# Loading the moved copies of the value rows two weight tiles later, with their tap products two splits further on, in a trunk kernel

## The chip, the cores and the metric

The kernel runs on one core of a Trainium2 chip, in one launch. The metric is the device time of that launch in microseconds; lower is better. A core has a matrix engine (TensorE, PE in the profile), a vector engine (VectorE, DVE), a scalar engine (ScalarE, ACT), GpSimd (POOL), and SyncE (SP), which here only issues transfers. Each engine works off its own instruction stream in order; where two engines depend on each other, a semaphore makes one wait. Transfers between the chip's main memory and the on-chip memory are issued by an engine into a queue and moved by 16 DMA engines.

## What is computed

One layer of a hybrid trunk for 256 tokens of width 2048. The parts that matter:

```python
proj = jnp.einsum('bsd,de->bse', rmsnorm(x, norm_mix_w[l]), w_in[l])
q, k, v, z, b_raw, a_raw, p_in, g_a, g_b = jnp.split(proj, splits, axis=-1)
qkv = jax.nn.silu(causal_dwconv(jnp.concatenate([q, k, v], axis=-1), conv_qkv_w[l]))
...
o = gated_delta_rule(q, k, v, g_log, beta)
o = rmsnorm(o, gdn_norm_w[l]) * jax.nn.silu(z.reshape(bsz, seq, N_HEADS, HEAD_DIM))
...
pooled = causal_multiscale_pool(p_in.reshape(bsz, seq, N_POOL_GROUPS, POOL_GROUP_DIM))
y_b = jnp.einsum('bsgc,gcd->bsgd', pooled, pool_w[l]).reshape(bsz, seq, D_POOL) * pool_scale[l]
mixed = jax.nn.sigmoid(g_a) * y_a + jax.nn.sigmoid(g_b) * y_b
x = x + jnp.einsum('bsd,de->bse', mixed, w_out[l])
```

After that comes a gated MLP (width 5632) with its own norms. The change touches the causal convolution of v: `causal_dwconv` over 4 taps is a sum of the rows of v, moved down by 0, 1, 2 and 3 tokens, each times its tap.

```python
def causal_dwconv(x, w):
    width = w.shape[0]
    seq = x.shape[1]
    xp = jnp.pad(x, ((0, 0), (width - 1, 0), (0, 0)))
    y = xp[:, 0:seq] * w[0]
    for j in range(1, width):
        y = y + xp[:, j:j + seq] * w[j]
    return y
```

## The kernel before

**Weights.** All large products read their weights in tiles of 256 x 512. A tile is loaded into `raw` (4 buffers, 512 KB each, SP's queue, L179), cast by ScalarE to its high half `whi` (L258), and VectorE subtracts that from the tile to get the low half `wlo` (L266). This subtraction is called the split; `splits` lists them in order, and "split 231" is the 231st. `whi` and `wlo` have 3 buffers each. `weights()` hands out a tile and begins the tile two further on; `last_load` is the most recent weight load.

**Gemms of the mixers.** `gemm_a` takes one tile at a time. For each it issues 12 matmuls on 128x512: high by high (L301), activations' low by weights' high (L302) and activations' high by weights' low (L303). After each half tile it calls `side()`, which takes one step of a generator, the side work. At the second tile of each gemm (`c == 1`) it first runs what stands in the list `later`.

**Order of the work.** The 16 heads are taken in 4 groups `g`. A group runs its gemms in this order: k, q, v, the pooling mixer's input (p), the gate GB, z and the pool product (in group 3 the pool product stands before z), and the gate GA; each is 8 tiles, the pool product 2. After the four groups comes the output projection. A scheduler that simulates the program decides the order of the instructions on each engine. It goes by the order in which the program states them and by readiness, with two exceptions: `tc.issue_after(x)` holds an instruction behind instruction x, and within `tc.manual_schedule` (from group 3's GA gemm to the output projection's first part) TensorE keeps the order in which the program states its work. In that stretch `ending` opens the last steps of group 3's side work.

**The value path.** `evict` (L714) copies a gemm's result from its bank to the tile `ev` (one buffer). The banks of `gemm_a`, `psm`, are two, taken in turn. For v, `ev` is written to memory (`vrow`, L1055). At the second tile of the next gemm, `v_moved` multiplies it by the last tap into `vt` (L735) and loads the three moved copies from `vrow` (L740): two take the buffers with the tag `cy`, which the convolutions of k and q also use, and one a buffer of its own, `mv`. Later `v_conv`, a part of the side work, multiplies each copy by its tap (L749) and adds it to `vt` (L750). Each product is held behind a split: the n-th behind the split with index `splits_of[g] + n`, and 3 later in group 0. `splits_of[g]` is the count of splits begun at the time of `v_moved`.

**The delta chain** (`gdn`, the side work of a group). Its steps, in order: decay differences (`crow`), Gram matrices on TensorE (L834, L836) with their diagonals (L839), the scaled blocks `ga0` and `ga1` (L853 to L858), their diagonal blocks out to memory (`cdd`, L872) and back (`lb`, L875), and a triangular solve in 31 steps on VectorE (L898, L900) with splits between. The result goes to memory (`tbd`, L905) and back (`TT`, L908), VectorE transposes it to `T` (L920), and TensorE reads it (L944). From there on come more products and merges, up to the group's output, which is gated (L1137, L1139), transposed (L346, copied to `mhi` and `mlo`) and kept as the output projection's operand. The steps of `v_conv` are the last of the side work before `T`, and the conv of q runs beside the first steps.

**The pooling mixer.** In group 3 the pooled values are made by 16 band matmuls (`banded`, L1072, L1074) from `ev`; ScalarE copies them to the high half `phi` (L1077) and VectorE makes the low half `plo` (L1078). They are what the pool product multiplies. `gate` (L1110) evicts a gate's gemm through a tanh, and `yb` (L1115) scales it.

Of the kernel before, what the change touches and what calls it, by code (L numbers as in the profile page):

```python
# [14 lines left out]
P = 128  # L15
S = 256
# [19 lines left out]
def kernel(  # L36
# [20 lines left out]
    nc = tc.nc  # L57
# [11 lines left out]
    def nm(s):  # L69
        cnt[0] += 1  # L70
        return f"{s}_{cnt[0]}"
# [90 lines left out]
    last_load = [None]  # L162
    last_split = [None]
    splits = []
    HALVES = 2

    def weights(ahead=AHEAD):

        begin(taken[0] + ahead + 1)
        taken[0] += 1  # L170
        return made[taken[0] - 1]
# [105 lines left out]
    def side():  # L277
        next(side_work[0], None)
# [5 lines left out]
    def pm():  # L284
        return psm.tile([P, 2, 512], F32, tag="m", name=nm("psm"))


    later = []

    def gemm_a(lh, ll, nk, steps=None, ps=None):  # L290

        ps = pm() if ps is None else ps
        for c in range(nk // 2) if steps is None else steps:
            if c == 1:
                while later:
                    later.pop(0)()
            hi, lo = weights()
            for kk in range(2):
                k = 2 * c + kk
                for t in range(2):  # L300
                    mm(ps[:, t, :], lh(k, t), hi[:, kk, :], start=(k == 0), stop=False)  # L301
                    mm(ps[:, t, :], ll(k, t), hi[:, kk, :], start=False, stop=False)  # L302
                    mm(ps[:, t, :], lh(k, t), lo[:, kk, :], start=False, stop=(k == nk - 1))  # L303
                side()
        return ps
# [395 lines left out]
    SH = 3  # L701
    vrow = dpool.tile([4, SH + S, 512], F32, tag="vrow", bufs=1, name="vrow")
# [28 lines left out]
    splits_of = {}  # L731

    def v_moved(e, g, vt):

        nc.vector.tensor_tensor(vt, e, taps_of[g][3], op=ALU.mult)  # L735
        moved_of[g] = []
        splits_of[g] = len(splits)
        for j in (1, 2, 3):
            m = mp.tile([P, 2, 512], F32, name=nm("mv"), **(dict(tag="cy", bufs=2) if j < 3 else dict(tag="mv")))
            nc.sync.dma_start(m, vrow[g, SH - j : SH - j + S, :].rearrange("(t p) d -> p t d", p=P))  # L740
            moved_of[g].append(m)

    def v_conv(g, vt):

        vt = vt.rearrange("p t h d -> p t (h d)")
        for n, (j, m) in enumerate(zip((2, 1, 0), moved_of[g])):

            with tc.issue_after(splits[splits_of[g] + n + (3 if g == 0 else 0)]):
                nc.vector.tensor_tensor(m, m, taps_of[g][j], op=ALU.mult)  # L749
            nc.vector.tensor_tensor(vt, vt, m, op=ALU.add)  # L750
            yield
        th = mp.tile([P, 2, 512], F32, tag="th", name=nm("th"))
        nc.scalar.activation(th, vt, AF.Tanh)
        yield
        nc.vector.scalar_tensor_tensor(vt, th, 1.0, vt, op0=ALU.add, op1=ALU.mult)
        yield
# [271 lines left out]
    for g in range(4):  # L1028
        kq = mp.tile([P, 4, 2, S], F32, tag="kq", bufs=1, name=nm("kq"))
        for kind, dst in ((1, kq[:, :, 0, :]), (0, kq[:, :, 1, :])):  # L1030
            ps = ps_k0 if kind == 1 and g == 0 else gemm_a(xh, xl, KD)
            e = evict(ps)
            convs.append(conv_silu(e, kind, g, dst))
            if g:
                later.append(lambda conv=convs[-1]: sum(1 for _ in conv))
            elif kind:

                later.append(lambda conv=convs[-1]: side_work.__setitem__(0, chain(conv, running_sums())))
            else:
                later.append(drain)  # L1040
# [3 lines left out]
        res = []  # L1044
        later.append(lambda g=g, kq=kq, vt=vt, res=res, conv=convs[-1]: side_work.__setitem__(
            0, along(gdn(g, kq, vt, v_conv(g, vt), res), conv)))
        v_taps(g)
        if g == 0:
# [3 lines left out]

            later.append(after_k)
        e = evict(gemm_a(xh, xl, KD), rsh)
        nc.sync.dma_start(vrow[g, SH : SH + S, :].rearrange("(t p) d -> p t d", p=P), e)  # L1055
        later.append(lambda e=e, g=g, vt2=vt2: v_moved(e, g, vt2))


        win = WINDOWS[g]
        psb = scales(g)  # L1060
        ps = gemm_a(xh, xl, KD)
        e = evict(ps) if g == 3 else evict(ps, rsh)
        phi = mtile(g, [P, 4, S], F32R, nm("phi"))
# [362 lines left out]
    def lh(k, t):  # L1426
        return at(hhi)(k, t)

    def ll(k, t):
        return at(hlo)(k, t)  # L1430
# [25 lines left out]
    for hf in range(2):  # L1456
# [11 lines left out]
        for n, step in enumerate(steps[hf]):  # L1468
# [11 lines left out]
            if step[0] == "plain":  # L1480
                kp, c = step[1], step[2] % 2
# [133 lines left out]
```

## Time and profile before

| | us |
|---|---|
| median of 3 runs | 1556.24 |
| lowest and highest of them | 1553.46, 1556.99 |
| profiled execution | 1555.57 |
| its span | 1553.9 |
| TensorE busy | 1537.2 |
| VectorE busy | 1195.2 |
| ScalarE busy | 828.8 |

The profile is that of one execution. A row of a timeline begins with the start and the duration in microseconds, then comes the engine, the line of the program, the operation, output and inputs, their shapes and how often it stands there in a row. Square brackets give the idle time before it on its engine and what ended it. In a group row, "x864 | 339.7, 393 | 1.4 <-DVE wlo L266 1.4" says that 864 instructions took 339.7 us, 393 ns each, and that the engine was idle for 1.4 us ahead of them, ended by VectorE's `wlo`. Matmuls are pipelined, so a matmul of 393 ns can be followed by the next one 0.23 us later. A row of the waits names the waiting engine and line, what it waited for, the total in microseconds, the times and the longest. A row of the chain of waits gives start, duration and what the end of the program hung on then. A row of the windows gives the stretch, its length, the engine's busy time and count, the granted clock of TensorE (1.00 is full), the DMA share and GB/s.

### The profile page before, as it was taken

The page shows a single profiled execution, that of the slowest core. Times are in us where ns is not written, and L with a number is a line of the kernel's source. Part 1 is how long each engine was busy: PE and PEld are TensorE (multiplying, and loading weights), DVE is VectorE, ACT ScalarE, POOL GpSimd, SP SyncE. Part 2 cuts the span into 40 slices and gives each one's busy share as a digit, 9 for nine tenths or more (in the row PEclk, how much of TensorE's full clock was granted, in tenths as well). Part 3 has the DMA queues.
Part 4 walks back from the last instruction along what each step waited for, and adds up shares of the span by engine and source line. Part 5 has one row for each costly group of instructions (what it writes and reads, how often), then busy time and mean ns, then how long its engine had stood idle before and what let it go on. Part 6 is the DMA issues. An engine that isn't in the chain of part 4 may idle for free.

```text
span 1553.9 us, 20103 instructions
## 1 busy us (share of the span) xinstructions
PE 1537.2 (99%) x7350; PEld 1268.1 (82%) x7350; DVE 1195.2 (77%) x1712; ACT 828.8 (53%) x1038; POOL 53.6 (3%) x66
## 2 busy tenths in 40 slices
PE   9999999999999999999999999999999999999998
PEld 8878888788878888888887888888888888788786
DVE  6789858996689858886665877777777776878775
ACT  6445446454545446454554656656666655555552
POOL 1010002000100000000000000000000000000000
PEclk9999999999999999999999999999999999999999
DMA  8777757776576756675667555556666558556562
GB/s 273 211 222 211 199 157 223 218 205 177 171 235 206 200 167 203 219 205 178 225 212 245 181 187 186 163 192 204 202 203 203 180 173 284 190 176 204 203 210 89
DMA packets 168018, 310.45 MB, mean 200 GB/s; under 512 B 19267, under 2 KB 23139, under 8 KB 167791
## 3 DMA queue, kind: packets, MB, share of 16 engines
q1 hardware_dynamic: 159456, 287.37, 59.9%
q0 software_dynamic: 3264, 12.58, 2.4%
q10 hardware_dynamic: 5198, 9.23, 1.9%
q8 instruction: 57, 0.93, 0.2%
q14 instruction: 43, 0.34, 0.1%
HBM read 301.75 MB, written 7.38 MB: 199 GB/s over the span
## 4 chain that ended last, share of the span: by engine, by line
PE 95%; DMA 2%; DVE 1%; issue 1%; ACT 1%; POOL 0%; POOLq 0%; ACTq 0%; DVEq 0%
PE psg L1324 29%; PE psm L303 14%; PE psm L301 14%; PE psm L302 14%; PE psm L1309 7%; PE psg L1309 6%; PE psm L444 1%; PE psm L1381 1%; PE psg L346 1%; PE psm L1324 1%; DMA vrow<-ev 1%; PE psg L834 1%; DVE wlo L266 1%; DMA mv<-vrow 1%; DMA raw<-in_w_down_dram 0%
## 5 line engine op out<-in xcount | busy, mean ns | idle before, releaser
L258 ACT CAST whi<-raw 128x1024 fp32r<-128x1024 f32 x460 | 483.9, 1053 | 482.0 <-PE psm L302 273.4
L266 DVE TENSOR_TENSOR wlo<-raw,whi 128x1024 fp32r<-128x1024 f32 x458 | 556.5, 1221 | 167.7 <-ACT whi L258 162.3
L303 PE MATMUL psm<-wlo,xhl 128*128 128x512 f32 x864 | 339.7, 393 | 1.4 <-DVE wlo L266 1.4
L301 PE MATMUL psm<-whi,xhl 128*128 128x512 f32 x864 | 338.6, 392 | 0.0
L302 PE MATMUL psm<-whi,xhl 128*128 128x512 f32 x864 | 337.9, 391 | 0.0
L1324 PE MATMUL psg<-whi,fhl 128*128 128x512 f32 x1208 | 302.1, 390 | 0.4 <-ACT whi L258 0.4
L1324 PEld LDWEIGHTS psg<-whi,fhl 128*128 128x128 f32 x1208 | 225.8, 188 | 47.4 <-ACT whi L258 1.2
L266 DVE TENSOR_TENSOR wlo<-quad,whi 128x1024 fp32r<-128x1024 f32 x112 | 137.1, 1224 | 75.4 <-ACT whi L258 72.1
L303 PEld LDWEIGHTS psm<-wlo,xhl 128*128 128x128 f32 x864 | 162.3, 188 | 35.7 <-DVE wlo L266 2.6
L302 PEld LDWEIGHTS psm<-whi,xhl 128*128 128x128 f32 x864 | 162.3, 188 | 33.4
L301 PEld LDWEIGHTS psm<-whi,xhl 128*128 128x128 f32 x864 | 162.3, 188 | 33.3 <-issue 0.2
L258 ACT CAST whi<-quad 128x1024 fp32r<-128x1024 f32 x112 | 118.1, 1055 | 105.0 <-PE psg L1324 55.9
L1324 PE MATMUL psg<-wlo,fhl 128*128 128x512 f32 x604 | 163.9, 389 | 0.0
L1324 PEld LDWEIGHTS psg<-wlo,fhl 128*128 128x128 f32 x604 | 113.4, 188 | 23.5
L1309 PE MATMUL psm<-wlo,hhi 128*128 128x512 f32 (+1 forms) x150 | 58.1, 387 | 1.1 <-DVE wlo L266 1.1
L1309 PE MATMUL psm<-whi,hhi 128*128 128x512 f32 (+1 forms) x150 | 58.1, 387 | 0.0
L1309 PE MATMUL psm<-whi,hlo 128*128 128x512 f32 (+1 forms) x150 | 57.9, 386 | 0.0
L198 DVE TENSOR_TENSOR quad<-quad 128x1024 f32<-128x1024 f32 x40 | 49.0, 1225 | 9.1 <-DMA quad<-in_w_up_dram 8.0
L1309 PE MATMUL psg<-whi,hhi 128*128 128x512 f32 (+1 forms) x130 | 50.4, 388 | 2.3 <-ACT whi L258 2.3
L301 PE MATMUL psm<-whi,mhi 128*128 128x512 f32 x128 | 50.9, 397 | 0.0
L1309 PE MATMUL psg<-whi,hlo 128*128 128x512 f32 (+1 forms) x130 | 50.2, 386 | 0.0
L303 PE MATMUL psm<-wlo,mhi 128*128 128x512 f32 x128 | 50.0, 390 | 0.0
(341 smaller groups left out, 1708.1 us busy)
## 6 DMA issues: line engine op xcount, KB each, us to landing
raw<-in_w_in_dram SPq DMA_DIRECT2D x224, 512.0 KB, 4.4
raw<-in_w_up_dram SPq DMA_DIRECT2D x136, 512.0 KB, 4.6
raw<-in_w_down_dram SPq DMA_DIRECT2D x64, 512.0 KB, 4.8
quad<-in_w_up_dram SPq DMA_DIRECT2D x40, 512.0 KB, 6.5
raw<-in_w_out_dram SPq DMA_DIRECT2D x32, 512.0 KB, 3.8
quad<-in_w_down_dram POOLq DMA_DIRECT2D x12, 1024.0 KB, 6.8
mv<-vrow SPq DMA_DIRECT2D x12, 512.0 KB, 4.6
taps<-in_conv_qkv_w_dram SPq DMA_DIRECT2D x16, 256.0 KB, 7.0
```

The costliest lines, as they stand in the source:

```text
L198: nc.vector.tensor_tensor(out_, plus_, minus_, op=ALU.subtract)
L258: nc.scalar.copy(hi, raw)
L266: last_split[0] = nc.vector.tensor_tensor(lo, raw, hi.bitcast(F32), op=ALU.subtract).ins
L301: mm(ps[:, t, :], lh(k, t), hi[:, kk, :], start=(k == 0), stop=False)
L302: mm(ps[:, t, :], ll(k, t), hi[:, kk, :], start=False, stop=False)
L303: mm(ps[:, t, :], lh(k, t), lo[:, kk, :], start=False, stop=(k == nk - 1))
L346: nc.tensor.transpose(pt[:, ff, t * P : (t + 1) * P], src[:, t, f * P : (f + 1) * P], ident)
L444: mm(ps_k0[:, t, :], part(k, t), w[:, kk, :], start=(k == 0 and w is hi and part is xh), stop=(k == KD - 1 and w is lo))
L834: mm(pg0, kq[:, h, 0, 0:P], kq[:, h, :, :], start=True, stop=True)
L1309: mm(ps[:, cs], lhs(kk), part_[:, kk, cs], start=(first and kk == 0 and n == 0), stop=(last and kk == 1 and n == 2), skip_group_check=shared)
L1324: mm(ps, lhs(kk), w[n][:, kk], start=(first and n == 0 and kk == 0 and lhs is high), stop=False, skip_group_check=True)
L1381: nc.tensor.transpose(out_[f // 2][:, f % 2, t * P : (t + 1) * P], e[:, t, f * P : (f + 1) * P], ident)
```

## The change

`gemm_a` gets a second list, `later_still`, that it runs at its fourth tile (`c == 3`). `v_moved` keeps the product with the last tap, and puts the three loads into this list, so that they are stated two tiles later; the count of splits is taken there too. Each load is now held behind the latest weight load. The products of `v_conv` stand behind the split with index `splits_of[g] + n + 2` in all groups, without the 3 of group 0.

```diff
     later = []
+    later_still = []
 
     def gemm_a(lh, ll, nk, steps=None, ps=None):
 
         ps = pm() if ps is None else ps
         for c in range(nk // 2) if steps is None else steps:
-            if c == 1:
-                while later:
-                    later.pop(0)()
+            if c in (1, 3):
+                due = later if c == 1 else later_still
+                while due:
+                    due.pop(0)()
...
         nc.vector.tensor_tensor(vt, e, taps_of[g][3], op=ALU.mult)
+        later_still.append(lambda: v_loads(g))
+
+    def v_loads(g):
+
         moved_of[g] = []
         splits_of[g] = len(splits)
         for j in (1, 2, 3):
             m = mp.tile([P, 2, 512], F32, name=nm("mv"), **(dict(tag="cy", bufs=2) if j < 3 else dict(tag="mv")))
-            nc.sync.dma_start(m, vrow[g, SH - j : SH - j + S, :].rearrange("(t p) d -> p t d", p=P))
+            with tc.issue_after(last_load[0]):
+                nc.sync.dma_start(m, vrow[g, SH - j : SH - j + S, :].rearrange("(t p) d -> p t d", p=P))
             moved_of[g].append(m)
...
-            with tc.issue_after(splits[splits_of[g] + n + (3 if g == 0 else 0)]):
+            with tc.issue_after(splits[splits_of[g] + n + 2]):
                 nc.vector.tensor_tensor(m, m, taps_of[g][j], op=ALU.mult)
```

## The prediction

> **What bounds the kernel now.** I read the page's first and fifth parts, then the list of waits, then the chain of waits around the third head group's copies, and last the timelines of the engines there and at the end of the head groups.
>
> ```profile
> PE 1537.2 (99%) x7350; PEld 1268.1 (82%) x7350; DVE 1195.2 (77%) x1712; ACT 828.8 (53%) x1038; POOL 53.6 (3%) x66
> ...
> L303 PE MATMUL psm<-wlo,xhl 128*128 128x512 f32 x864 | 339.7, 393 | 1.4 <-DVE wlo L266 1.4
> ```
>
> TensorE is busy for 99% of the span. So an edit that moves only vector work and transfers can gain no more than the few waits of TensorE that they cause, and loses whatever new wait it gives TensorE. The waits that touch this change:
>
> ```profile
> DVE mv L749 <- DMA mv<-vrow: 11.4, 5, 4.4
> ...
> DVE T L920 <- DMA TT<-tbd: 8.2, 4, 2.2
> ...
> PE psm L1212 <- DVE fhl L1218: 2.5, 1, 2.5
> ...
> PE psm L303 <- DVE wlo L266: 1.4, 2, 1.1
> ```
>
> VectorE stands 11.4 us for the copies (`mv`). TensorE stands for it in only two places. The chain of waits shows how the longest comes about, and the timelines (VectorE, ScalarE, TensorE) what each piece took:
>
> ```profile
> 442.11 6.25 DMA vrow<-ev
> 448.38 3.62 DMA mv<-vrow
> ...
> 459.34 1.15 DVE wlo L266
> 460.54 0.50 PE psm L303
> ```
>
> ```profile
> 452.02 1.22 DVE L749 TENSOR_TENSOR mv<-mv,taps 128x1024 f32<-128x1024 f32 x1 [4.37 <-DMA mv<-vrow]
> ...
> 459.26 1.22 DVE L266 TENSOR_TENSOR wlo<-raw,whi 128x1024 fp32r<-128x1024 f32 x1
> 453.37 1.06 ACT L258 CAST whi<-raw 128x1024 fp32r<-128x1024 f32 x1 [4.30 <-PE psm L302]
> 281.02 0.39 PE L302 MATMUL psm<-whi,xhl 128*128 128x512 f32 x1
> 281.77 0.50 PE L303 MATMUL psm<-wlo,xhl 128*128 128x512 f32 x1 [0.37 <-DVE wlo L266]
> 459.07 0.39 PE L302 MATMUL psm<-whi,xhl 128*128 128x512 f32 x1
> 460.54 0.50 PE L303 MATMUL psm<-wlo,xhl 128*128 128x512 f32 x1 [1.08 <-DVE wlo L266]
> ```
>
> VectorE waits 4.37 us for the first copy, then works off products and sums, and the split that TensorE needs begins at 459.26, though its high half was ready at 454.43. TensorE's matmuls of this shape start 0.23 us apart in the chain's run, so from 459.07 to 460.54 it loses 1.47 − 0.23 = 1.24 us, and from 281.02 to 281.77 another 0.52. The matmul after each stall starts about 0.1 us late. That is 1.76 to 2.0 us in all, and it is all that the copies cost. The split at 459.26 was done at 460.48, which is 4.8 us after an undisturbed one (454.43 + 1.22 = 455.65); 1.24 of it stalled TensorE, so a split may be 3.6 us late for nothing.
>
> **The change part by part.** *Loads later, products later.* The three loads leave behind later weight tiles, one by one, and the products stand one split further back in group 0 and four in the other groups (two tiles for the later count, and two by the new offset, less the 3 that group 0 had). By the instruction order of the changed program every product has at least two splits between its load and itself. I take VectorE's first-copy wait as gone, and with it both stalls: **−1.8 us** (0 to −2.0). The loads and products themselves cost the same and lie beside TensorE.
>
> *What else moves.* Steps of the delta chain stand behind these products on VectorE. In the instruction order of the changed program the Grams, the decay blocks, the triangular solve and its transfers all come later: by 2 splits in group 0, 5 in group 1, 5 to 6 in group 2 and 3 to 5 in group 3. In groups 0 to 2 the matmuls that read the result move back with them (the first one from tile 116.5 to 121.75 in group 1), so nothing waits. In group 3 TensorE's order is fixed by hand from the last gate gemm on: there the matmuls at L944 stay at the same place in the order of the tiles, and only what feeds them is later. The last solve step moves from behind split 228 to behind split 231. The rows of before (VectorE, SP's queue, ScalarE and TensorE):
>
> ```profile
> 707.22 0.18 DVE L900 TENSOR_TENSOR tb<-tb,tmp 128x8 f32<-128x8 f32 x1
> 707.42 1.73 SPq L905 DMA_DIRECT2D tbd<-tb  x4
> 711.16 1.80 SPq L908 DMA_DIRECT2D TT<-tbd  x4
> 713.97 1.84 DVE L920 STREAM_TRANSPOSE T<-TT 32x256 f32<-32x256 f32 x4 [1.86 <-DMA TT<-tbd]
> 712.52 1.05 ACT L258 CAST whi<-raw 128x1024 fp32r<-128x1024 f32 x1 [1.67 <-PE psm L302]
> 716.40 0.39 PE L303 MATMUL psm<-wlo,xhl 128*128 128x512 f32 x1
> 716.72 0.69 PE L944 MATMUL psg<-T,ga 32*32 32x32 f32 x32
> ```
>
> From the end of the solve (707.40) out to memory, back as `TT` and through the transposes (end 715.81) are 8.41 us, and the matmul at 716.72 finds it with 0.9 us to spare. After the change the last solve step stands behind the split of the tile whose high half is cast from 712.52 to 713.57. That split takes 1.22, so it ends at 714.8, and the one step behind it at about 714.9. The same 8.41 us later it is 723.3, where TensorE is due at 716.72: it waits **6.6 us** (6.1 if the first matmul needs only three of the four transposes, which are 0.46 each; 7.2 if the two transfers meet weight loads). Nothing covers this: all that TensorE has in its order after the L944 matmuls stands behind them. On SP's queue `tbd` now follows the weight load that the same split frees, and `TT` one load more, which is free (717.5) before `tbd` has landed (718.6, by the 3.74 us between the two rows), so the queue adds nothing.
>
> *The last pool gemm.* The band matmuls of group 3 (L1072, L1074) move from 5 tiles ahead of the pool gemm to right in front of it, and the pool gemm reads what is made from them, `phi` (ScalarE) and `plo` (VectorE):
>
> ```profile
> 656.93 0.59 ACT L1077 CAST phi<-psg 128x512 fp32r<-128x512 f32 x1 [2.38 <-PE psg L1074]
> ...
> 657.55 0.69 DVE L1078 TENSOR_TENSOR plo<-psg,phi 128x512 fp32r<-128x512 f32 x1 [0.84 <-ACT phi L1077]
> L1115 DVE SCALAR_TENSOR_TENSOR yb<-gate,psb x4: 1214/1220/1220, 139.5 to 671.9; 128x1024 f32<-128x1024 f32 x4
> 655.80 0.38 PE L1072 MATMUL psg<-bands,ev 128*128 128x128 f32 x2
> 657.58 0.48 PE L302 MATMUL psm<-whi,xhl 128*128 128x512 f32 x1
> 669.03 0.39 PE L301 MATMUL psm<-whi,phi 128*128 128x512 f32 x1
> 720.11 1.27 ACT L1110 ACTIVATE gate<-psm,rsh 128x512 f32<-128x512 f32 x2
> ```
>
> The gate gemm before it ends at 669.0, the band matmuls take 1.8 (655.80 to 657.58), so TensorE would be ready at 670.8. In the changed order ScalarE does a cast (1.05), the gate (1.27) and then `phi` (0.59); VectorE does `yb` (1.22) after the gate and then `plo` (0.69). From 669.2 that is 670.25, 671.5, 672.7 and 673.4: TensorE waits **2.7 us**. If the gate and `yb` had been done first, it would be `phi` and `plo` behind the first half of the band matmuls, some 0.9 us; I keep 0.9 to 2.9 and take the upper value, since the order puts those steps first.
>
> *Bank and splits.* The transposes that free the `ev` tile for q's eviction move to one tile (2.7 us) ahead of the gemm that needs q's bank in group 3, and to 1.25 tiles (3.4 us) in group 2:
>
> ```profile
> 419.82 0.71 PE L346 MATMUL psg<-ident,ev 128*128 128x128 f32 x5
> 423.67 1.28 ACT L714 ACTIVATE ev<-psm,rs 128x512 f32<-128x512 f32 x2
> 600.76 0.93 PE L346 MATMUL psg<-ident,ev 128*128 128x128 f32 x7
> 602.31 1.29 ACT L714 ACTIVATE ev<-psm,rs 128x512 f32<-128x512 f32 x2
> ```
>
> From the transposes' end to the eviction's end these take 1.9 us (group 3) and 4.4 us (group 2), so each place costs 0 to 1.7 us. VectorE's queue between the products of groups 2 and 3 is also denser; a split that comes 2 to 5 us late, against the 3.6 free ones, costs 0 to 1.4 in each. Together 0 to 6; I take 1.0, near the lower end, since in group 3 the row leaves 0.8 us and since only one split of before went past its slack by over 1 us.
>
> *The clock.* A wait of 6.6 us is longer than any that TensorE has in the middle of before. The granted clock in windows of TensorE, and the longest wait:
>
> ```profile
> 822.00:830.00 8.00, 5.53 (x29) 1.00 0.86 249
> 1549.50:1553.90 4.40, 0.00 (x0) 0.50 0.59 213
> 1546.20:1549.40 3.20, 0.00 (x0) 1.00 0.06 24
> 827.24 0.66 PE L1212 MATMUL psm<-ident,xt 128*128 128x128 f32 x4 [2.47 <-DVE fhl L1218]
> ```
>
> After the last matmul the clock stays at 1.00 for the first 3.2 us and is 0.50 from 1549.5 on. The wait of 2.47 us left it at 1.00. So a wait of 6.6 us would drop it to half, and the work after it starts slow. How long, no row shows; the stretch at half clock lasts 4.4 us without an end, and that long at half pace costs 2.2 us. I take **1.4** between 0 and 2.2. [...]
>
> **Sum**, against the profiled execution's 1555.57 us: −1.8 + 6.6 + 2.7 + 1.0 + 1.4 = +9.9, so 1565.5. The median of the three runs shown is 0.7 us higher, 1556.24, so 1566.1 on that; between the two I say **1565.8 us**. The bounds of the terms give −2.0 + 6.1 + 0.9 + 0 + 0 = +5.0 (1561) and 0 + 7.2 + 2.9 + 6 + 2.2 = +18.3 (1574), and all at one end is unlikely.
>
> **The rivals.**
> *Only the wait in group 3.* The pool gemm's operands come in time, the bank and the splits cost nothing, and the clock holds: −1.8 + 6.6 = +4.8, so 1561. For it: before has only two stalls by splits in some 230 tiles. Against it: the order of the band matmuls.
> *Hidden, not slower.* The solve of group 3 is done in time after all. It would have to be over by 716.72 − 8.41 = 708.3, so its split would have to run 6.6 us earlier against TensorE. The high half of that tile begins when TensorE releases a buffer (the 1.67 us wait for L302 in the row at 712.52), which speaks against it. Then −1.8 is left: 1554.4, within what can be told from no change; if the other stalls are also cheaper than I see, nothing of it is slower.
> *Waits pile up.* VectorE falls behind: the copies are late again behind weight loads, splits in groups 2 and 3 come over 3.6 us late, and q's bank is late: the upper bound of these places, +5 on the sum, 1571. For it: the loads now share SP's queue with weight loads in front of them; against it: VectorE is idle for 23% of the span.
> *The clock holds.* The fall sets in only where TensorE gets no instruction at all, and the wait at L944 doesn't lower it: 1565.8 − 1.4 = 1564.4. For it: the only fall of before is after the last matmul; against it: nothing in the windows tells a waiting from a finished engine.
>
> **How the numbers follow.** The forecast with a fall of the clock 0.52, the same with the clock held 0.12, only the wait 0.13, piling up 0.15, hidden 0.08. The forecast's own range is 1562 to 1570. The range reaches down to the wait alone less the first matmul's half microsecond and the spread of the runs, and up past the piling up: 1559 to 1573. About 0.2%, or 3.1 us, is what a measurement of this kernel can tell from no change. The hidden case gives −1.8, so it falls within it: within 0.07, faster by more 0.03 (the hidden case with a better run than shown), slower 0.90.
>
> **What would show it.** In the profile of the changed kernel: the stalls of L303 at 281 and 460 are gone, and VectorE's wait for `mv` is below 3 us; TensorE waits about 6.6 us for `T` in front of L944's line, some 10 us after the place where it stands now; it waits 2 to 3 us for `phi` or `plo` at the last pool gemm; the granted clock is below 1.00 in the microseconds after the long wait. The prediction would be wrong if TensorE meets `T` without a wait, or if new waits of over 3 us lie elsewhere.

## The result and the profile after

The changed kernel takes 1565.95 us (median of 4 runs, 1564.53 to 1565.98), the kernel before 1555.84 us beside it (4 runs). The ratio is 1.0067, with a 95% interval of 1.0054 to 1.0079: slower by 0.67%. The profiled execution after took 1564.53 us with a span of 1562.8, which is 8.96 us over the profiled one of before.

The page of the changed kernel, its first and fifth parts (the program's lines behind L297 are 2 higher than before, those behind L735 are 7 higher):

```profile
PE 1540.1 (99%) x7350; PEld 1269.9 (81%) x7350; DVE 1195.1 (76%) x1712; ACT 828.0 (53%) x1038; POOL 44.4 (3%) x66
...
L305 PE MATMUL psm<-wlo,xhl 128*128 128x512 f32 x864 | 339.9, 394 | 0.8 <-DVE wlo L266 0.8
```

TensorE is busy for 2.9 us more, though it has the same 7350 instructions: some of them were slower. The rest of the loss is idle time. The waits of TensorE and one of VectorE's in the changed kernel (total, times, longest):

```profile
PE psg L951 <- DVE T L927: 6.4, 2, 5.7
...
PE psm L305 <- DVE wlo L266: 0.8, 2, 0.4
PE psm L303 <- ACT phi L1084: 0.7, 1, 0.7
```

```profile
DVE mv L756 <- DMA mv<-vrow: 3.1, 2, 2.8
```

VectorE's wait for the copies went from 11.4 to 3.1 us, as the change has it. In its place TensorE has a wait for `T` that was not there before. Its stretch of the timeline in the changed kernel, VectorE first, then SP's queue, then TensorE:

```profile
713.43 1.22 DVE L266 TENSOR_TENSOR wlo<-raw,whi 128x1024 fp32r<-128x1024 f32 x1 [0.32 <-ACT whi L258]
714.57 0.17 DVE L907 TENSOR_TENSOR tb<-tb,tmp 128x8 f32<-128x8 f32 x1
...
721.86 1.84 DVE L927 STREAM_TRANSPOSE T<-TT 32x256 f32<-32x256 f32 x4 [4.48 <-DMA TT<-tbd]
```

```profile
715.10 1.86 SPq L912 DMA_DIRECT2D tbd<-tb  x4
...
719.11 1.80 SPq L915 DMA_DIRECT2D TT<-tbd  x4
```

```profile
716.22 0.39 PE L305 MATMUL psm<-wlo,xhl 128*128 128x512 f32 x1
722.34 0.31 PE L951 MATMUL psg<-T,ga 32*32 32x32 f32 x2 [5.73 <-DVE T L927]
723.28 1.06 PE L951 MATMUL psg<-T,ga 32*32 32x32 f32 x30 [0.62 <-DVE T L927]
...
724.71 0.77 PE L303 MATMUL psm<-whi,xhl 128*128 128x512 f32 x1
725.28 0.63 PE L304 MATMUL psm<-whi,xhl 128*128 128x512 f32 x1
...
731.23 0.69 PE L969 MATMUL psg<-U,TT 32*32 32x32 f32 x32
```

The last solve step ends at 714.74, the transposes at 723.70. TensorE stood at this point at 716.72 before; now it starts at 722.34, has two products, and waits once more. The matmuls after that start 0.43 to 0.57 us apart, where 0.23 is usual. The windows of TensorE there show why (us, busy, granted clock, DMA share, GB/s):

```profile
716.20:719.00 2.80, 0.41 (x2) 1.00 0.74 231
719.00:720.00 1.00, 0.00 (x0) 0.64 0.93 293
720.00:724.00 4.00, 1.03 (x30) 0.50 0.32 74
724.00:729.00 5.00, 5.00 (x24) 0.50 0.01 3
729.00:730.00 1.00, 1.00 (x4) 0.74 0.03 8
730.00:732.00 2.00, 2.00 (x39) 1.00 0.56 170
```

The clock falls to half about 3 us into the wait (the mean of 0.64 puts the fall at 719.3) and is back at 729.5 (the mean of 0.74), some 5 us after TensorE has its large matmuls again. So the ledger of the two profiles is short. At the last matmul in front of the wait the changed kernel is 0.18 us ahead (716.22 against 716.40). At the next group of 32x32 products (721.89 before, in the row below, and 731.23 after) it is 9.34 us behind. At the last matmul it is 8.97 behind (1545.84 and 1554.81). The whole loss lies in 15 us.

```profile
721.89 0.69 PE L962 MATMUL psg<-U,TT 32*32 32x32 f32 x32
```

### The profile page after: what moved, and what is told of

The parts are those of the page before. It is cut to its first block, busy times and chain, and to the rows that moved or that the text cites. A ratio compares the mean times of both kernels' runs of the same rounds, so it can differ in the third digit from the quotient of the medians.

```text
span 1562.8 us, 20117 instructions
## 1 busy us (share of the span) xinstructions
PE 1540.1 (99%) x7350; PEld 1269.9 (81%) x7350; DVE 1195.1 (76%) x1712; ACT 828.0 (53%) x1038; POOL 44.4 (3%) x66
## 4 chain that ended last, share of the span: by engine, by line
PE 94%; DMA 2%; DVE 1%; issue 1%; ACT 1%; SPq 1%; POOL 0%; POOLq 0%; DVEq 0%; ACTq 0%
PE psg L1331 28%; PE psm L303 14%; PE psm L305 14%; PE psm L304 14%; PE psm L1316 7%; PE psg L1316 6%; PE psm L446 1%; PE psm L1388 1%; PE psg L841 1%; PE psm L1331 1%; PE psg L348 1%; DMA lb<-cdd 1%; DMA raw<-in_w_up_dram 1%; DVE wlo L266 1%; DMA raw<-in_w_down_dram 0%
## 5 line engine op out<-in xcount | busy, mean ns | idle before, releaser
L304 PE MATMUL psm<-whi,mlo 128*128 128x512 f32 x128 | 50.4, 393 | 0.0
```

## The experiments

All ratios are against the kernel before, run on the same chip. Experiments 1 to 4, 5 to 8 and 9 to 11 ran on three different chips, so medians are compared within these groups, and ratios across them.

**1. The whole change, but group 0's products one split earlier.**

```diff
-            with tc.issue_after(splits[splits_of[g] + n + 2]):
+            with tc.issue_after(splits[splits_of[g] + n + (1 if g == 0 else 2)]):
```

> The whole change, but group 0's three products stand one split earlier, where they stood before; the loads stay two tiles later in all groups, and groups 1 to 3 keep the change in full. Theory A (one split more in group 0 makes the delta chain late from group to group, so that T of group 3 comes 6.6 us late): the wait for T in front of the 32x32 products is gone, with it the half clock, and the time is 1553.5 to 1556.5 us. Theory B (each group's own later products make its own chain late): group 3 keeps its four splits, so the wait for T stays and the time is 1563 to 1567 us. Theory C (the later loads make the chain late): also 1563 to 1567 us.

1554.51 us against 1554.66, ratio 1.0002 (0.9993 to 1.0010). Theories B and C fall: groups 1 to 3 have the change in full, and the products find `T` in time. TensorE in this kernel:

```profile
473.83 1.03 PE L348 MATMUL psg<-ident,ev 128*128 128x128 f32 x8
476.07 0.50 PE L305 MATMUL psm<-wlo,xhl 128*128 128x512 f32 x1 [1.22 <-DVE wlo L266]
...
718.19 0.69 PE L951 MATMUL psg<-T,ga 32*32 32x32 f32 x32
```

There is no wait in front of L951. But there is no gain either: the stalls at 281 and 460 are gone, and others are there, the largest at 474 to 476, where VectorE had a product, a sum and six steps of the decay blocks between two splits. Where VectorE waited for a copy, it now has work that was put off.

**2. The products alone, the loads where they were.**

```diff
-            with tc.issue_after(splits[splits_of[g] + n + (3 if g == 0 else 0)]):
+            with tc.issue_after(splits[splits_of[g] + n + 4]):
```

> The kernel before with the products alone at the changed kernel's splits (index n + 4 counted from the old place); the loads stay at the second tile. Theory A: the late chain comes from the products, so the wait for T of about 6.6 us and the half clock are there: 1564 to 1567 us. Theory C (the loads): no wait for T, 1554 to 1557 us.

1563.59 us, ratio 1.0062 (1.0050 to 1.0075). This is the wait for `T` again without the later loads, and experiment 1 had the later loads without the loss. So the loads play no part in it. The median lies 0.4 us under the expected range. TensorE's wait and VectorE's wait for the copies in this kernel:

```profile
PE psg L944 <- DVE T L920: 6.4, 2, 5.8
```

```profile
DVE mv L749 <- DMA mv<-vrow: 2.4, 1, 2.4
```

VectorE waits no longer for the copies than in the changed kernel: later products alone hide the transfer, and moving the loads adds nothing that shows.

**3. Group 0's products alone, one split later.**

```diff
-            with tc.issue_after(splits[splits_of[g] + n + (3 if g == 0 else 0)]):
+            with tc.issue_after(splits[splits_of[g] + n + (4 if g == 0 else 0)]):
```

> The kernel before with group 0's products one split later (4 in place of 3) and nothing else. The solve of group 1 then ends one split later and that of groups 2 and 3 where it did, so the late chain is caught up when the later groups have their products early. Theory A: no wait for T in group 3, 1555 to 1557.5 us. If one split in group 0 were enough for all of it: 1564 to 1567 us.

1556.42 us, ratio 1.0011 (1.0001 to 1.0020), and no wait for `T`. One split in group 0 is needed for the loss (experiment 1), and it is not enough for it.

**4. The change in groups 0 and 1, groups 2 and 3 as before.**

```diff
+        if g in (0, 1):
+            later_still.append(lambda: v_loads(g))
+        else:
+            v_loads(g)
...
-            with tc.issue_after(splits[splits_of[g] + n + 2]):
+            with tc.issue_after(splits[splits_of[g] + n + (2 if g in (0, 1) else 3 if g == 0 else 0)]):
```

> The change in groups 0 and 1 alone; groups 2 and 3 load and multiply as before. Theory A (group 0's delay is handed on, and group 1's later products keep it from being caught up): the last solve step of group 3 is three splits later, though its own products are as before, and TensorE waits about 6.6 us for T: 1564 to 1567 us. Theory B (each group's own products): 1554 to 1557 us, no wait for T.

1566.04 us, ratio 1.0077 (1.0064 to 1.0089). Group 3's own products and loads are those of the kernel before, and TensorE waits for its `T` all the same:

```profile
PE psg L954 <- DVE T L930: 7.0, 2, 6.4
...
PE psg L348 <- ACT ev L716: 1.5, 1, 1.5
```

How the delay is handed on can be seen at the casts of `mhi`, the end of the chain of groups 0, 1 and 2. ScalarE's rows in the kernel before, in the changed kernel, in experiment 3 and in experiment 4:

```profile
242.07 1.08 ACT L1162 CAST mhi<-psg 128x512 fp32r<-128x512 f32 x2 [0.18 <-PE psg L346]
422.00 1.05 ACT L1162 CAST mhi<-psg 128x512 fp32r<-128x512 f32 x2
600.63 1.08 ACT L1162 CAST mhi<-psg 128x512 fp32r<-128x512 f32 x2 [0.29 <-PE psg L346]
```

```profile
249.04 1.07 ACT L1169 CAST mhi<-psg 128x512 fp32r<-128x512 f32 x2 [2.21 <-PE psg L348]
434.80 1.08 ACT L1169 CAST mhi<-psg 128x512 fp32r<-128x512 f32 x2 [2.10 <-PE psg L348]
612.86 1.08 ACT L1169 CAST mhi<-psg 128x512 fp32r<-128x512 f32 x2
```

```profile
249.17 1.07 ACT L1162 CAST mhi<-psg 128x512 fp32r<-128x512 f32 x2 [2.21 <-PE psg L346]
425.14 1.07 ACT L1162 CAST mhi<-psg 128x512 fp32r<-128x512 f32 x2
599.28 1.08 ACT L1162 CAST mhi<-psg 128x512 fp32r<-128x512 f32 x2 [0.18 <-PE psg L346]
```

```profile
248.95 1.07 ACT L1172 CAST mhi<-psg 128x512 fp32r<-128x512 f32 x2 [2.21 <-PE psg L348]
434.06 1.07 ACT L1172 CAST mhi<-psg 128x512 fp32r<-128x512 f32 x2 [2.11 <-PE psg L348]
614.73 1.07 ACT L1172 CAST mhi<-psg 128x512 fp32r<-128x512 f32 x2
```

Group 0's end is 7 us late in all three. With groups 1 to 3 as before the delay shrinks to 3 us and then to nothing. With group 1's products later as well it grows to 12 to 14 us and stays, even if groups 2 and 3 are left alone. How one split, 2.7 us, becomes 7 us at the end of group 0 these runs don't show. In the program's order the transposes of a group's gated output stand ahead of the transposes of the next group's k, so the next group's Grams, solve and `T` start from there. That it is this order that hands the delay on is read from the program and the instruction order; no run took it away.

**5, 6 and 9. What the wait itself and the clock cost.** The changed kernel once more, as a base:

> The changed kernel once more, as the base for the next run. All theories: 1564.5 to 1566.5 us, with the wait of about 6.6 us for T and the half clock for some 5 us after it.

1565.16 us (5 runs), ratio 1.0065 (1.0053 to 1.0078). In this profile the wait for `T` is 7.3 us in all, where the first profile of the same kernel has 6.4 (between 710 and 730 TensorE is busy for 12.65 us here and for 13.65 there), so the wait differs by about a microsecond from one execution to another. Then with extra matmuls in front of the 32x32 products of group 3:

```diff
+        if g == 3:
+            warm = pg()
+            rows = mhi[0][:, 0:2, :].rearrange("p a s -> p (a s)")
+            for _ in range(26):
+                mm(warm, xh(0, 0), rows, start=True, stop=True)
```

> The changed kernel with 26 extra matmuls of 128x512 in front of group 3's first 32x32 products; they read an operand of the output projection that is there already, and nobody reads what they write. At 0.2275 us each they fill 5.9 us of the wait for T. Theory clock (TensorE is slow after the wait because it was idle): the granted clock stays at 1.00, the 2.5 us of slow matmuls after the wait are gone, and the time is 1562.5 to 1564 us. Rival (the matmuls after the wait are slow for want of operands): the time stays at 1565 to 1566.5 us; if the extra matmuls outlast the wait it grows.

1563.94 us (1560.72 to 1565.32), ratio 1.0053 (1.0040 to 1.0066), 1.2 us under the base. The clock did not stay up as expected; the windows of this kernel:

```profile
714.00:725.00 11.00, 9.49 (x72) 1.00 0.45 132
725.00:729.00 4.00, 4.00 (x12) 0.58 0.01 2
```

The extra matmuls ended at 721.8, and the products with `T` began at 722.52 (two of them) and 723.55 (the other thirty). That left two gaps of 0.7 and 0.8 us, and some 2 us after the second the clock fell. So 33 instead of 26:

> The changed kernel with 33 instead of 26 extra matmuls in front of group 3's 32x32 products: 7.5 us, so that they reach to the end of the wait for T (the wait with 26 left two gaps of 0.7 and 0.8 us, and the clock still fell for 3.3 us). Theory clock by recent work (the fall follows from a stretch with little work, wherever it lies): no gap of over 0.3 us is left there, the granted clock stays at 1.00 from 714 to 732, and the time is 1561.5 to 1563.5 us, some 2 us under the changed kernel. Rival (the fall is set off by something else than idle time, such as the 32x32 products): the clock falls to 0.50 again and the time is 1563.5 to 1566 us.

1563.03 us (1561.99 to 1566.77), ratio 1.0053 (1.0040 to 1.0066), the same ratio as with 26; by the ratios this is 1.9 us under the base. The intervals of the three overlap, so the times alone don't settle it; the profile of this kernel does for the clock:

```profile
714.00:732.00 18.00, 17.95 (x137) 1.00 0.39 118
```

```profile
716.22 7.64 PE L950 MATMUL psg<-mhi,xhl 128*128 128x512 f32 x33
723.79 0.98 PE L956 MATMUL psg<-T,ga 32*32 32x32 f32 x32
```

With no gap the clock stays at 1.00 and the matmuls after the products are 0.23 us apart again. From the start of the 32x32 products to the next group of them it takes 5.45 us here, 8.89 in the changed kernel and 5.17 in the kernel before. The slow matmuls came from the idle time, not from missing operands.

**7. The kernel before with group 3's solve late, and nothing else.**

```diff
-LATE = (26, 24, 22, 18)
+LATE = (26, 24, 22, 28)
```

> The kernel before with 10 more half-tile steps in front of group 3's triangular solve and nothing else: its last step then stands behind the same split as in the changed kernel, three later than before. Theory A: this alone is the loss, the wait for T of 6.6 us plus 2.5 us at half clock on the time of before: 1563 to 1566 us. Rival (the loss is made up of many small waits of the later chain in groups 0 to 2): under 1560 us.

1563.84 us, ratio 1.0059 (1.0047 to 1.0072). One late `T` makes as large a loss as the whole change. TensorE's wait and windows in this kernel (its profile is that of its slowest run, 1566.14 us, in which the stall by a split at 460 is also 0.7 us longer than before):

```profile
PE psg L944 <- DVE T L920: 6.5, 2, 5.8
```

```profile
720.00:724.00 4.00, 0.31 (x2) 0.59 0.59 157
724.00:730.00 6.00, 5.63 (x42) 0.50 0.01 3
```

**8, 10 and 11. Can it be made faster than before?** First the products of groups 1 and 2 one split later than in the kernel before, which leaves the solve where it was:

```diff
-            with tc.issue_after(splits[splits_of[g] + n + (3 if g == 0 else 0)]):
+            with tc.issue_after(splits[splits_of[g] + n + (3, 1, 1, 0)[g]]):
```

> The kernel before with the products of groups 1 and 2 one split later and nothing else (groups 0 and 3 and all loads as before). The order changes only there: in group 1 one split goes ahead of the second product, in group 2 the third product goes behind one more split. Theory A: the solve stays where it was, both stalls of TensorE (0.5 and 1.2 us) go, and the time is 1 to 2 us below the kernel before. Rival (VectorE is full there, so the split that goes ahead only makes another one late, as where group 0 alone was put back): within 0.7 us of the kernel before.

1555.41 us against 1554.88, ratio 1.0004 (0.9995 to 1.0013). In its profile (1552.97 us, its fastest run) TensorE has no wait for a split of the in-projection at all, but the median shows no gain, so the rival's number came true, though its reason, another split made late, doesn't show in this profile. The stalls are not gone in every execution: in the profile of experiment 11, which has the same products one split later, splits stop TensorE for 0.3 us at 149 and 0.6 us at 463. How much of the missing gain this accounts for the runs don't settle. Another thing that varies from run to run is seen in the profiles, at 825 us, where TensorE waits 2.47 us in every kernel up to here. The windows in the kernel before and in experiment 1:

```profile
827.00:831.00 4.00, 3.76 (x19) 1.00 0.82 239
```

```profile
828.00:832.00 4.00, 3.31 (x11) 0.57 0.73 195
```

The same wait drops the clock in one execution and not in the other: of the eleven profiles with this wait, it fell in those of experiments 1, 3 and 9. So this wait was filled with 10 extra matmuls, in the kernel before and with the repair of experiment 8:

```diff
+                if c == 3 and k2 == 0:
+                    warm = pg()
+                    full = both(fhl, 0)
+                    with tc.issue_after(last):
+                        for _ in range(10):
+                            mm(warm, full[:, 0, 0:P], full.rearrange("p a s -> p (a s)"), start=True, stop=True)
```

> The kernel before with 10 extra matmuls of 128x512 in the wait of 2.5 us at 825 us (between the two halves of the last transposes in front of the MLP); nobody reads their result. Of the profiles so far, two that were taken with this wait show a granted clock of 0.9 in the 20 us after it and the others 1.00, so the same wait seems to drop the clock in some runs and not in others. Theory clock: with the wait filled, no run loses the 1.8 us; the median is 0.5 to 1.5 us under the kernel before and the runs lie closer together than its 1552 to 1557 us. Rival (the spread of the runs has another cause): the same median within 0.5 us and the same spread, or up to 0.5 us longer by the extra work.

> The kernel before with the products of groups 1 and 2 one split later (which took both of TensorE's stalls away) and the 10 extra matmuls at 825 us. If both repairs are worth what they look like (1.8 us, and the fall of the clock in some runs): 1552 to 1553.5 us. If neither is to be told from the spread of the runs: 1554 to 1556 us.

1554.73 us, ratio 0.9999 (0.9990 to 1.0008), and 1554.28 us, ratio 0.9998 (0.9989 to 1.0006), against 1555.14. Neither is to be told from the kernel before. In both profiles the clock stays at 1.00 from 825 to 1540, but it did so in eight of the eleven with the wait as well. The spread did not shrink as the theory had it (1553.36 to 1558.82 and 1553.89 to 1557.83, where the kernel before has 1553.27 to 1557.43), so this wait is not shown to be what makes the runs differ. No version beats it by more than its spread.

## Why the prediction was right, and where it was off

The time (1565.8 predicted, 1565.95 measured) and its main cause came out. Not all of the terms did: the clock cost 1.6 us more than I had put, the last pool gemm about 1.8 us less, and the two errors cancel. That the number fits to 0.2 us is luck.

- **The wait for T, 6.6 us: right.** TensorE starts the products 5.62 us later than before and waits another 0.6 to 0.7 us inside them (the 0.62 of the row, 0.72 by the spacing); with the 0.18 us by which it was ahead, the wait is 6.5 us. The solve ended at 714.74 (predicted 714.9) and the transposes at 723.70 (723.3). The path between took 8.96 us instead of 8.41, 0.34 of it because the weight load in front of `tbd` was issued only at 714.68, and most of the rest between `tbd` and `TT` (4.01 us instead of 3.74). I had said that the queue adds nothing. Against that, the first two products needed only the first of the four transposes, and the others began at 723.28, before the last had ended. In the other profile of this kernel (experiment 5) the wait is 7.3 us, so a fit to a tenth is more than the estimate can claim. Experiment 7 shows that a late `T` with its clock is enough for a loss of this size.
- **Its cause: right for the mechanism in group 3, wrong for where it comes from.** I wrote that the chain's steps "stand behind these products on VectorE" and gave the delays group by group, as if each group's products made its own. Experiments 1, 3 and 4 show that group 3's own products make none. The delay begins with the one split in group 0, group 1's later products keep it from being caught up, and it is handed on.
- **The clock, 1.4 between 0 and 2.2: the direction right, the size too small.** From the start of the 32x32 products to the next group of them it took 8.89 us (722.34 to 731.23), where it took 5.17 before (716.72 to 721.89). Less the second wait of 0.7 that is 3.0 us. Half of the seen 4.4 us, which I used as a bound, was no bound: the stretch at half clock reached from 719.3 to 729.5, and the work from 722.3 on lay in it. No row of before shows the 1.4 itself; it was my estimate between the bounds, and the runs showed 3.0 in its place.
- **The copies, −1.8: right.** Both stalls are gone. (New ones by splits came elsewhere; see below.)
- **The last pool gemm, 2.7: a mis-sized step.** It measured 0.85 to 1.0. TensorE in the changed kernel, then ScalarE:

```profile
668.67 0.50 PE L303 MATMUL psm<-whi,phi 128*128 128x512 f32 x1 [0.67 <-ACT phi L1084]
669.02 0.40 PE L303 MATMUL psm<-whi,xhl 128*128 128x512 f32 x1
```

```profile
666.89 1.26 ACT L1117 ACTIVATE gate<-psm,rsh 128x512 f32<-128x512 f32 x2
668.04 1.07 ACT L1084 CAST phi<-psg 128x512 fp32r<-128x512 f32 x2
```

  ScalarE's steps came in the order that I had read: a cast from 665.93 on, the gate, `phi`. But TensorE went on when the first half of `phi` was there, and after one product with it TensorE's order turns to z's gemm, so nobody waits for the other half or for `plo`. I had TensorE wait until `plo`, behind all steps of ScalarE and VectorE in full. (By the figures of the prediction, 673.4 less 670.8, that is 2.6.)
- **Bank and splits, 1.0 in groups 2 and 3: nearly right in size by luck, wrong in place.** Neither the bank nor a split of groups 2 and 3 stopped TensorE. Splits stopped it in groups 0 and 1:

```profile
142.38 0.39 PE L304 MATMUL psm<-whi,xhl 128*128 128x512 f32 x1
143.20 0.50 PE L305 MATMUL psm<-wlo,xhl 128*128 128x512 f32 x1 [0.42 <-DVE wlo L266]
...
322.92 0.39 PE L304 MATMUL psm<-whi,xhl 128*128 128x512 f32 x1
323.67 0.50 PE L305 MATMUL psm<-wlo,xhl 128*128 128x512 f32 x1 [0.36 <-DVE wlo L266]
```

  By the spacing these cost 0.59 and 0.52 us, 1.3 with the late matmul behind each. The bank's wait did show in experiment 4, with 1.5 us for the eviction of `ev`.
- **The rivals.** "Only the wait" and "piling up" fall with the ledger: nearly all of the loss lies between 716 and 731. "Hidden" was the case of experiments 1 and 3, where the solve of group 3 is over in time. "The clock holds" falls with the windows.
- **The signs.** The stalls at 281 and 460 are gone, TensorE waits for `T`, the clock is below 1.00 after it, and no other new wait is over 3 us. VectorE's wait for the copies is 3.1 us, not below 3, and TensorE's wait for `phi` is 0.7, not 2 to 3. The products with `T` start 5.6 us after their old place, not some 10; the prediction's own terms ahead of them add up to 8.5 (−1.8 + 6.6 + 2.7 + 1.0).

Up to 716 the terms make −2.0 + 1.0 + 1.3 = +0.3, and the profiles show −0.2; the half microsecond between is spread over small differences that I can't name. Behind 824 us the changed kernel gets 0.3 back; from the wait at that point to the last matmul the two profiles of the changed kernel (the first and that of experiment 5) also differ by 0.3.

## What to carry to other kernels

Before a step is moved, look for the consumer whose place is fixed. Where the scheduler may move the consumer along, a delay need cost nothing: in groups 0 to 2 the chain ended 7 to 13 us later and TensorE never waited for `T`. At the one place where the order is written by hand, the delay came out as a wait. A delay in an early round of a loop can reach the last round though that round was not touched, so try the change round by round. And a wait of TensorE can cost more than its length: after the 6.5 us here the work began at half clock (0.50), for another 3.0 us.

## What the runs showed of the hardware

The clock fell in the changed kernel from 1.00 to 0.50 about 3 us into the wait, and came back some 5 us after the large matmuls went on, which cost 3.0 us on top of a wait of 6.5. After a wait of 2.47 us it fell in three of eleven profiles (to 0.57 from 828 to 832 in experiment 1) and not in the others (1.00 from 827 to 831 before). In experiment 6 it fell some 2 us after two gaps of 0.7 and 0.8 us around two small products (0.58 from 725 to 729); in experiment 9, without the gaps, the same products left it at 1.00. Why the same wait of 2.47 us goes either way, no run here shows.
